# A trunk layer on one core: two output-projection blocks run together, and two norms moved into the middle of feed-forward blocks

## The chip, the cores and the metric

The kernel runs on one core of a Trainium2 chip. The metric is the device time of one execution in microseconds (us), the median over several runs. The core has five engines that work side by side, each through its own instructions in a fixed order: TensorE (PE) multiplies matrices, VectorE (DVE), ScalarE (ACT) and GpSimd (POOL) do elementwise work, and SyncE (SP) issues most of the transfers (DMA) between the chip's memory and the core's own.

## The reference, cut to what matters

The layer mixes three branches into `merged`, projects it, and adds the normed result to `x`; a second norm feeds a gated feed-forward network with a causal convolution of width three. The change touches the last lines of the mixer and the first ones of the network:

```python
def rms_norm(x, g):
    y = x * lax.rsqrt(jnp.mean(x * x, axis=-1, keepdims=True) + NORM_EPS)
    return y * g

merged = gates[:, :, 0] * y_pool + gates[:, :, 1] * y_rwkv + gates[:, :, 2] * y_mem
x = x + rms_norm(merged @ w_o[l], norm_mix_post[l])          # projection, residual norm
h = rms_norm(x, norm_ffn_pre[l])                             # next norm
u = causal_dwconv(h @ w_ffn_up[l], conv_w[l], conv_b[l])     # feed-forward, up
u_gate, u_val = jnp.split(u, 2, axis=-1)
f = (jax.nn.gelu(u_gate, approximate=True) * u_val) @ w_ffn_down[l]
x = x + rms_norm(f, norm_ffn_post[l])
```

The sequence has 1024 rows, `x` has 1024 channels, the feed-forward has 2 x 2816.

## The kernel before, in words

All activations lie transposed: 128 channels on the partitions, 512 positions (a half of the sequence) in a row. A product of float32 accuracy is made of three matmuls on a high and a low part of both factors (`mm3`, lines 163 to 171: the lines L168, L169 and L170 of the profile). A block of 128 output channels for one half takes 8 rows of the contraction (`k` = 0 to 7), so 24 matmuls (`gemm`).

Each block's weights come in four tiles of two `k` each (`load_more`): SP issues a load into a raw buffer (L158), ACT casts it to the high part `whi` (L129), and POOL subtracts to get the low part `wlo` (L132). Blocks take turns between two classes of buffers, each with three raw and four split tiles, so that a block's fourth load has to wait until the first tile's raw buffer has been split. The tile scheduler fixes the order on every engine when the program is built. An engine that waits holds up all that stands behind it, and SP likewise holds up later loads.

The stretch of the program around the change, in order:

- `merge(0)` makes the eight merged rows of the first half. Its last step for a row is a cast by ACT (`mgh`, L122) and a subtraction by DVE (`mgl`, L123).
- `wo_gemm(0)` makes the eight projection blocks of the first half, one after the other. Each reads all eight merged rows, the last one made last.
- `merge(1)`, the residual step and norm of the first half, and `wo_gemm(1)` for the second half follow. `wo_gemm(1)` runs its first two blocks through `two_gemms`: rows 0 to 6 of both, then row 7 of both.
- Then come the feed-forward blocks of the first half. This text calls the first ten of them U0 to U9: channels 0, NF, 1, NF+1, 2, NF+2, 3, NF+3, 4, NF+4 (NF = 22; the ones below NF are gates, `ug`, the others values, `uv`). Each block's result is convolved by one ACT pass (L962) and two DVE passes (L963, L964, with a small copy, L966).
- Between them runs the second half's residual step. `wo_residual(1)` sums squares over channels by a matmul with a matrix of ones (`psn<-ss`, L1148), takes the reciprocal root by two ACT passes (Ln and Exp, L200), and then on each of eight rows `o` DVE scales (L1191), adds `x` (L1193) and, with a square by ACT (L1139, L1142), accumulates the next sum of squares `s2` (L1143); SP stores the row to `d_x1` (L1194). Before, the matmul of this norm stands behind U0.
- `wo_norm(1)` does the same with `s2`: matmul (`psn<-s`, L1148), Ln, Exp, and on each row a scaling by DVE (L1210) and a split into `h2h` and `h2l`. Before, its matmul stands behind U5. Behind it ACT loads its table for gelu (L194), and `up_act` makes gelu times value for the finished pairs and stores them.
- Then come U10 and on: the first blocks of the second half, beside which DVE and ACT make differences and splits of the two halves (`differences`, L1306, L122, L123) that the remaining channels need. Those run as pairs with fewer products (`up_pairs`), followed by the down projection.

Of the kernel before, what the change touches and what calls it, by code (L numbers as in the profile page):

```python
# [20 lines left out]
KC = D // P  # L21
# [7 lines left out]
NF = 22  # L29
# [15 lines left out]
def trunk_kernel(ctx: ExitStack, tc: tile.TileContext, xT, memT, pvec, w_in, w_kv, w_upd, w_upg,  # L45
# [76 lines left out]
        A.copy(hi, src)  # L122
        return (lo_eng or V).tensor_tensor(lo, src, hi.bitcast(F32), op=ALU.subtract)  # L123

    hi_on_act, lo_on_dve, last_whi = [False], [False], [None]

    def split_w(src, hi, lo):
        if hi_on_act[0]:
            last_whi[0] = A.copy(hi, src).ins  # L129
        else:  # L130
            G.tensor_scalar(hi, src, 1.0, 0.0, op0=ALU.mult, op1=ALU.add)
        (V if lo_on_dve[0] else G).tensor_tensor(lo, src, hi.bitcast(F32), op=ALU.subtract)  # L132
# [11 lines left out]
    def load_w(ap, nk, kp=2, c=None):  # L144
        if c is None:
            cls[0] ^= 1
            c = cls[0]
        ps = Ws()
        ps.c = c
        for k0 in range(0, nk, kp):  # L150
            load_more(ps, ap, k0, min(kp, nk - k0), kp)
        return ps
# [17 lines left out]
        last_mm[0] = PE.matmul(ps, wl, xh, start=False, stop=stop).ins  # L170
        return first

    def gemm(ws, rhs, width=512, behind=None, ps=None, log=None):

        if ps is None:
            ps = psg.tile([P, 512], F32, name="psg", tag=f"g{getattr(ws, 'c', 0)}")[:, :width]
        n = len(ws)
        for k in range(n):
            m = mm3(ps, ws[k], rhs(k), k == 0, k == n - 1)
            if k == 0 and behind is not None:  # L180
                later(m, behind)
            if log is not None:
                log.append(last_mm[0])
        return ps


# [6 lines left out]
    def table(name):  # L193
        load = A.preload_act_table_set(name).ins  # L194
        for u in phase[1]:
            tc.add_manual_dep(load, u.name, nosync, reason="table")
        phase[:] = [load, [load]]
# [759 lines left out]
    def conv(j, n, src, d):  # L957

        if n == 0:
            zcs[j] = const.tile([P, 2], F32, name="zc2", tag="zc2", bufs=16)  # L960
        zc = zcs[j]
        A.activation(d, src, AF.Identity, scale=col("cw2", j), bias=col("cb", j))  # L962
        V.scalar_tensor_tensor(d[:, 1:], src[:, :511], col("cw1", j), d[:, 1:], op0=ALU.mult, op1=ALU.add)  # L963
        V.scalar_tensor_tensor(d[:, 2:], src[:, :510], col("cw0", j), d[:, 2:], op0=ALU.mult, op1=ALU.add)  # L964
        if n == 0:
            V.tensor_copy(zc, src[:, 510:512])  # L966
        else:
            V.scalar_tensor_tensor(d[:, 0:1], zc[:, 1:2], col("cw1", j), d[:, 0:1], op0=ALU.mult,
                                   op1=ALU.add)
            V.scalar_tensor_tensor(d[:, 0:2], zc, col("cw0", j), d[:, 0:2], op0=ALU.mult, op1=ALU.add)  # L970
# [4 lines left out]
        cnt[e] = (cnt[e] + 1) % 4  # L975
        return pmp.tile([P, 512], F32, name=name, tag=f"n{8 + 4 * e + cnt[e]}")

    def up_block(j, n, ws):
        e = j // NF
        d = work(e, ("ug", "uv")[e])  # L980
        conv(j, n, gemm(ws, lambda k: (h2h[n][:, k], h2l[n][:, k])), d)
        return d

    def up_act(i, n, ug, uv):
# [172 lines left out]
    def wo_gemm(n, js):  # L1157
        s = slice(n * 512, n * 512 + 512)
        for j in js:
            if j == 0:  # L1160
                o = [(ow if n == 0 else ow1).tile([P, 2, 512], F32, name="o", tag=f"q{4 * n + a}") for a in range(4)]
                os_.append([o[k // 2][:, k % 2] for k in range(KC)])
                sss.append(ow.tile([P, 512], F32, name="ss", tag="ss", bufs=2))
            rhs = lambda k: (mgh[k][:, s], mgl[n][k])
            if n == 1 and j == 0:
                two.extend(two_gemms([load_w(w_o[e], KC) for e in range(2)], rhs, KC - 1))
            ps = two.pop(0) if two else gemm(load_w(w_o[j], KC), rhs)
            V.tensor_copy(os_[n][j], ps)
            if n == 1 and j > 4:
                sq = wp.tile([P, 512], F32, name="sq", tag="st", bufs=3)  # L1170
                V.tensor_tensor(sq, os_[n][j], os_[n][j], op=ALU.mult)
                V.tensor_tensor(sss[n], sss[n], sq, op=ALU.add)
            else:
                sumsq(sss[n], ps, j == 0, V)

    def wo_residual(n, after=None):

        s = slice(n * 512, n * 512 + 512)
        o = os_[n]
        rs = norm(ow, sss[n], after)  # L1180
        s2 = ow.tile([P, 512], F32, name="s2", tag="ss", bufs=2)
        if n:
            xts = hf.tile([P, KC, 512], F32, name="xts", tag="h2h1")
            SP.dma_start(xts, xT[:, s].rearrange("(k p) t -> p k t", p=P))
        for k in range(KC):
            if n:
                xt = xts[:, k]
            else:
                xt = ow.tile([P, 512], F32, name="xt", tag="xt", bufs=2)
                SP.dma_start(xt, xT[k * P:(k + 1) * P, s])  # L1190
            V.scalar_tensor_tensor(o[k], o[k], col("g_mix_post", k), rs, op0=ALU.mult,  # L1191
                                   op1=ALU.mult)
            V.tensor_tensor(o[k], o[k], xt, op=ALU.add)  # L1193
            SP.dma_start(d_x1[k][:, s], o[k])  # L1194
            sumsq(s2, o[k], k == 0, V)
            if k % 2:
                yield s2
# [6 lines left out]
    def wo_norm(n, s2, after=None):  # L1204

        o = os_[n]
        rs = norm(ow, s2, after)
        new_h2()
        for k in range(KC):
            V.scalar_tensor_tensor(o[k], o[k], col("g_ffn_pre", k), rs, op0=ALU.mult,  # L1210
                                   op1=ALU.mult)
            split(o[k], h2h[n][:, k], h2l[n][:, k], V)
            if k % 2:
                yield
# [24 lines left out]
    for _ in wo_norm(0, s2, last_mm[0]):  # L1239
        pass  # L1240
    wo_gemm(1, range(2, 8))
    def first(j):
        return up_block(j, 0, load_w(w_fup[j], KC))

    pairs = [[first(0)]]
    res = wo_residual(1, last_mm[0])
    s2 = next(res)
    pairs[0].append(first(NF))
    s2 = next(res)
    for i in (1, 2):  # L1250
        pairs.append([first(i)])
        s2 = next(res, s2)
        pairs[i].append(first(NF + i))
        s2 = next(res, s2)

    ahead = [load_w(w_fup[3], KC), load_w(w_fup[NF + 3], KC)]
    steps = wo_norm(1, s2, last_mm[0])
    next(steps)
    table(GELU)
    later(phase[0], last_whi[0], True)  # L1260
    for n in range(4):
        j = (3, NF + 3, 4, NF + 4)[n]
        d = up_block(j, 0, ahead.pop(0))
        if n < 2:
            ahead.append(load_w(w_fup[(4, NF + 4)[n]], KC))
            up_act(n, 0, *pairs[n])
            pairs.append([d])
        else:
            up_act(n, 0, *pairs[n]) if n == 2 else None
            pairs.append([d])  # L1270
        if n < 3:
            next(steps)
    up_act(3, 0, pairs[3][0], pairs[4][0])
    up_act(4, 0, pairs[5][0], pairs[6][0])


    o0, o1 = os_
# [389 lines left out]
```

## Time and profile before

| what | value |
|---|---|
| median of 3 runs | 2056.73 us (2052.93 to 2056.75) |
| the profiled execution's own time | 2058.67 us |
| span of its profile | 2056.8 us |
| mean granted clock of TensorE | 0.995 |
| merged rows of the first half, last subtraction ends | 1241.37 us |
| projection blocks of the first half, first matmul | 1232.85 us |
| U0, first matmul | 1371.35 us |
| matmul of the second half's residual norm | 1376.79 us |
| matmul of its next norm | 1408.79 us |

The profile is one execution. A row of the timeline gives the start in us from the span's start, the duration, engine, line, operation and tiles; `x4` merges four equal instructions in a row, and brackets give the engine's idle time before it and what ended that. A row of the table by stretches gives the stretch's length, then for each engine its busy time and number of instructions, the share of its clock that TensorE was granted (PEclk), and the DMA share and rate. Busy time of PE overstates, because matmuls overlap: their rate is read from their starts.

### The profile page before, as it was taken

What the parts mean: (1) busy time and instruction counts of PE and PEld (TensorE: products, weight loads), DVE (VectorE), ACT (ScalarE), POOL (GpSimd) and SP (SyncE); (2) the same over time, 40 slices, a digit from 0 to 9 for tenths busy, and PEclk for the clock granted to TensorE, in tenths of its full rate; (3) what the DMA queues carried; (4) which work ended last, traced back from release to release, by engine and by line L of the source; (5) the groups of instructions that cost most, each with busy time, mean ns of one, the idle gap of its engine ahead of it and who ended that gap; (6) DMA issues with size and microseconds to landing.
All of it is one profiled execution on the core that took longest, in us unless ns stands there. A gap on an engine that the chain in (4) does not pass through costs nothing. (4 is left out here: it accounts for less than half of the span.)

```text
span 2056.8 us, 34070 instructions
## 1 busy us (share of the span) xinstructions
PE 2000.2 (97%) x12246; PEld 1558.2 (76%) x12246; DVE 1378.4 (67%) x2204; ACT 1073.6 (52%) x2249; POOL 804.4 (39%) x883
## 2 busy tenths in 40 slices
PE   8999999999999999999999999999999999999997
PEld 5777767786778667776778887877678888877886
DVE  6567537663568357734596552768889888867798
ACT  7575338723773358434567343545544554444544
POOL 4521213121222121111122355655579888832441
PEclk9999999999999999999999999999999999999999
DMA  4412112120212121212525543645332222169776
GB/s 152 136 42 75 66 36 86 58 93 22 88 62 83 36 90 40 90 63 89 193 92 189 157 136 106 191 129 164 97 95 87 85 80 82 67 198 260 166 183 150
DMA packets 176714, 221.84 MB, mean 108 GB/s; under 512 B 16544, under 2 KB 128288, under 8 KB 176544
## 3 DMA queue, kind: packets, MB, share of 16 engines
q1 hardware_dynamic: 163616, 204.44, 30.7%
q0 software_dynamic: 11856, 14.16, 4.2%
q8 instruction: 97, 1.59, 0.3%
q10 hardware_dynamic: 1072, 1.05, 0.2%
q14 instruction: 73, 0.60, 0.1%
HBM read 170.30 MB, written 49.28 MB: 107 GB/s over the span
## 5 line engine op out<-in xcount | busy, mean ns | idle before, releaser
L132 POOL TENSOR_TENSOR wlo<-wraw,whi 128x256 fp32r<-128x256 f32 x472 | 412.7, 884 | 940.7 <-ACT whi L129 774.5
L168 PE MATMUL psg<-hh,whi 128*128 128x512 f32 x928 | 380.1, 410 | 2.6 <-DVE kv L315 2.6
L170 PE MATMUL psg<-hh,wlo 128*128 128x512 f32 x928 | 376.3, 406 | 0.4
L169 PE MATMUL psg<-hl,whi 128*128 128x512 f32 x928 | 375.5, 405 | 0.0
L129 ACT CAST whi<-wraw 128x256 fp32r<-128x256 f32 x472 | 182.5, 403 | 227.6 <-PE psg L169 105.7
L168 PEld LDWEIGHTS psg<-hh,whi 128*128 128x128 f32 x928 | 174.6, 188 | 43.1 <-DVE kv L315 3.8
L170 PEld LDWEIGHTS psg<-hh,wlo 128*128 128x128 f32 x928 | 174.2, 188 | 43.2 <-POOL wlo L132 5.9
L169 PEld LDWEIGHTS psg<-hl,whi 128*128 128x128 f32 x928 | 174.6, 188 | 39.4 <-issue 3.6
L1011 POOL TENSOR_TENSOR wt<-a,wt 128x256 fp32r<-128x256 f32 x136 | 156.7, 1176 | 35.6 <-ACT wt L1010 35.6
L168 PE MATMUL psd<-f,u 128*128 128x512 f32 x292 | 114.7, 393 | 3.1 <-ACT u L1405 2.4
L169 PE MATMUL psd<-f,u 128*128 128x512 f32 x292 | 114.6, 393 | 0.6 <-DVE f L1409 0.6
L170 PE MATMUL psd<-f,u 128*128 128x512 f32 x292 | 114.1, 392 | 0.0
L170 PE MATMUL psf<-h2h,wt 128*128 128x512 f32 x272 | 105.9, 389 | 1.0 <-POOL wt L1011 1.0
L169 PE MATMUL psf<-h2l,wt 128*128 128x512 f32 x272 | 105.8, 389 | 0.0
L168 PE MATMUL psf<-h2h,wt 128*128 128x512 f32 x272 | 105.8, 389 | 0.0
L1025 DVE SCALAR_TENSOR_TENSOR d<-z,pv,d 128x1023 f32<-128x1023 f32 x68 | 101.1, 1491 | 2.2
L1011 POOL TENSOR_TENSOR wt<-s,wt 128x256 fp32r<-128x256 f32 x68 | 80.3, 1201 | 3.4 <-ACT wt L1010 2.1
L686 DVE TENSOR_TENSOR HV<-ph,Hd 64x128 f32<-64x128 f32 x112 | 32.4, 289 | 72.2 <-PE ph L640 48.1
L168 PE MATMUL psf<-t,wt 128*128 128x512 f32 x204 | 79.4, 389 | 0.0
L169 PE MATMUL psf<-t,wt 128*128 128x512 f32 x204 | 79.4, 389 | 0.0
L170 PE MATMUL psf<-t,wt 128*128 128x512 f32 x204 | 79.4, 389 | 0.0
L1023 ACT ACTIVATE d<-z,pv 128x1024 f32<-128x1024 f32 x34 | 42.4, 1246 | 67.6 <-DVE z L1102 51.9
(425 smaller groups left out, 4747.0 us busy)
## 6 DMA issues: line engine op xcount, KB each, us to landing
wraw<-in_w_in SPq DMA_DIRECT2D x240, 128.0 KB, 2.4
a<-in_w_fup SPq DMA_DIRECT2D x128, 128.0 KB, 2.4
d_zg<-st SPq DMA_DIRECT2D x48, 256.0 KB, 2.7
wraw<-in_w_fup SPq DMA_DIRECT2D x80, 128.0 KB, 2.5
fw<-in_w_fdn SPq DMA_DIRECT2D x33, 256.0 KB, 4.3
fraw<-d_f SPq DMA_DIRECT2D x33, 256.0 KB, 4.5
wraw<-in_w_prwkv SPq DMA_DIRECT2D x64, 128.0 KB, 2.4
wraw<-in_w_o SPq DMA_DIRECT2D x64, 128.0 KB, 2.5
```

The costliest lines, as they stand in the source:

```text
L129: last_whi[0] = A.copy(hi, src).ins
L132: (V if lo_on_dve[0] else G).tensor_tensor(lo, src, hi.bitcast(F32), op=ALU.subtract)
L168: first = PE.matmul(ps, wh, xh, start=start, stop=False)
L169: PE.matmul(ps, wh, xl, start=False, stop=False)
L170: last_mm[0] = PE.matmul(ps, wl, xh, start=False, stop=stop).ins
L686: ready = V.tensor_tensor(HV[q, :, c + 1, e], ph[q], Hd[q], op=ALU.add).ins
L1011: low = eng.tensor_tensor(w[1][:, us], src[u], w[0][:, us].bitcast(F32), op=ALU.subtract)
L1023: A.activation(d, z, AF.Identity, scale=col("cw2", j), bias=col("cb", j))
L1025: V.scalar_tensor_tensor(d[:, n:], z[:, :T - n], col(cw, j), d[:, n:], op0=ALU.mult, op1=ALU.add)
```

## The change

Three things are moved:

1. `wo_gemm(0)` now also takes its first two blocks through `two_gemms`: rows 0 to 6 of both, then row 7 of both.
2. The matmul of the second half's residual norm stands in the middle of U0 (behind the fourth of its eight rows) and that of the next norm in the middle of U5. All that hangs on them is recorded from there: the residual rows are spread over U0 to U4, and `up_act` and the steps of `wo_norm` come one block earlier.
3. Two sets of weight casts are pinned behind the norms on ACT (`hold`): those of U2 behind the Exp of the first norm, those of U7 behind the Exp of the second. The pin of the gelu table behind the last weight cast is gone.

In the changed file lines from 126 on stand three lines lower, and those from 188 on five lower: L200 becomes L205, L1148 becomes L1153.

```diff
-            last_whi[0] = A.copy(hi, src).ins
+            i = A.copy(hi, src)
+            last_whi[0] = i.ins
+            if hold[0] is not None:
+                later(i, hold[0])
...
-    def gemm(ws, rhs, width=512, behind=None, ps=None, log=None):
+    def gemm(ws, rhs, width=512, behind=None, ps=None, log=None, amid=None):
...
+            if amid is not None and k == 3:
+                amid()
...
-            if n == 1 and j == 0:
+            if j == 0:
                 two.extend(two_gemms([load_w(w_o[e], KC) for e in range(2)], rhs, KC - 1))
...
-    pairs = [[first(0)]]
-    res = wo_residual(1, last_mm[0])
-    s2 = next(res)
-    pairs[0].append(first(NF))
-    s2 = next(res)
-    for i in (1, 2):
-        pairs.append([first(i)])
-        s2 = next(res, s2)
-        pairs[i].append(first(NF + i))
-        s2 = next(res, s2)
-
-    ahead = [load_w(w_fup[3], KC), load_w(w_fup[NF + 3], KC)]
-    steps = wo_norm(1, s2, last_mm[0])
-    next(steps)
-    table(GELU)
-    later(phase[0], last_whi[0], True)
+    def begin():
+        res.append(wo_residual(1, last_mm[0]))
+        s2[0] = next(res[0])
+        pins.append(phase[1][-1])
+
+    def end():
+        steps.append(wo_norm(1, s2[0], last_mm[0]))
+        next(steps[0])
+        pins.append(phase[1][-1])
+        table(GELU)
+
+    res, steps, pins = [], [], []
+    first(0, begin)
+    for j in (NF, 1, NF + 1, 2):
+        s2[0] = next(res[0], s2[0])
+        hold[0] = pins[0] if j == 1 else None
+        first(j)
+
+    queue = (NF + 2, 3, NF + 3, 4, NF + 4)
+    ahead = [load_w(w_fup[j], KC) for j in queue[:2]]
+    for n, j in enumerate(queue):
+        blocks.append(up_block(j, 0, ahead.pop(0), None if n else end))
         if n < 3:
-            next(steps)
-    up_act(3, 0, pairs[3][0], pairs[4][0])
-    up_act(4, 0, pairs[5][0], pairs[6][0])
+            hold[0] = None if n else pins[1]
+            ahead.append(load_w(w_fup[queue[n + 2]], KC))
+            hold[0] = None
+            up_act(n, 0, *blocks[2 * n:2 * n + 2])
+            next(steps[0])
+    for n in (3, 4):
+        up_act(n, 0, *blocks[2 * n:2 * n + 2])
```

What the scheduler makes of it is shown by the order of instructions at three places. On PE, before, the first two projection blocks of the first half meet like this (`psg_12561` is the first block's accumulator, `psg_12612` the second's; `mgh7` and `mgl70` are the last merged row):

```order
L170 MATMUL psg_12561<-mgh6_12071,wlo_12557 128x512
L168 MATMUL psg_12561<-mgh7_12072,whi_12556 128x512
L169 MATMUL psg_12561<-mgl70_12529,whi_12556 128x512
L170 MATMUL psg_12561<-mgh7_12072,wlo_12557 128x512
L168 MATMUL psg_12612<-mgh0_12065,whi_12589 128x512
```

On PE, after, with `psg_12585` and `psg_12586` for the two blocks, the end of the second block's row 6 and the two last rows:

```order
L173 MATMUL psg_12586<-mgh6_12071,wlo_12581 128x512
L171 MATMUL psg_12585<-mgh7_12072,whi_12556 128x512
L172 MATMUL psg_12585<-mgl70_12529,whi_12556 128x512
L173 MATMUL psg_12585<-mgh7_12072,wlo_12557 128x512
L171 MATMUL psg_12586<-mgh7_12072,whi_12580 128x512
L172 MATMUL psg_12586<-mgl70_12529,whi_12580 128x512
L173 MATMUL psg_12586<-mgh7_12072,wlo_12581 128x512
```

The last merged row is first read after 42 matmuls and no longer after 21. On ACT, before, the Ln and Exp of the second half's residual norm (`rs`) stand behind eight weight casts, four of U1 (`whi_14026` to `whi_14044`) and four of U2 (`whi_14093` to `whi_14111`), and behind the convolution pass of U0:

```order
L129 CAST whi_14038<-wraw_14037 128x256
L129 CAST whi_14044<-wraw_14043 128x256
L129 CAST whi_14093<-wraw_14092 128x256
L129 CAST whi_14099<-wraw_14098 128x256
L129 CAST whi_14105<-wraw_14104 128x256
L129 CAST whi_14111<-wraw_14110 128x256
L962 ACTIVATE ug_13976<-psg_13977,pv_83 128x512
L200 ACTIVATE rs_14009<-psn_14007,eps_111 128x512
L200 ACTIVATE rs_14009<-rs_14009 128x512
```

On ACT, after, U1's four casts are `whi_14038` to `whi_14056` and U2's first three `whi_14105` to `whi_14117`:

```order
L129 CAST whi_14050<-wraw_14049 128x256
L129 CAST whi_14056<-wraw_14055 128x256
L205 ACTIVATE rs_13992<-psn_13990,eps_111 128x512
L205 ACTIVATE rs_13992<-rs_13992 128x512
L129 CAST whi_14105<-wraw_14104 128x256
L129 CAST whi_14111<-wraw_14110 128x256
L129 CAST whi_14117<-wraw_14116 128x256
L967 ACTIVATE ug_13976<-psg_13977,pv_83 128x512
```

U2's casts and U0's convolution now stand behind the Exp; U1's fourth cast still stands ahead of the Ln. At the second norm on ACT, before, the last cast ahead is U7's fourth (`whi_14379`), and U5's convolution (`uv_14305`) stands ahead too:

```order
L129 CAST whi_14379<-wraw_14378 128x256
L962 ACTIVATE uv_14305<-psg_14306,pv_83 128x512
L200 ACTIVATE rs_14386<-psn_14384,eps_111 128x512
L200 ACTIVATE rs_14386<-rs_14386 128x512
L194 ACT_TABLE_LOAD
```

On ACT, after, `whi_14324` is U6's fourth cast, `ug_14250` U4's convolution, `uv_14329` U5's, and `whi_14375` U7's first cast:

```order
L129 CAST whi_14324<-wraw_14323 128x256
L967 ACTIVATE ug_14250<-psg_14251,pv_83 128x512
L205 ACTIVATE rs_14345<-psn_14343,eps_111 128x512
L205 ACTIVATE rs_14345<-rs_14345 128x512
L199 ACT_TABLE_LOAD
L122 CAST h2h1_14348<-o_13493 128x512 x2
L967 ACTIVATE uv_14329<-psg_14330,pv_83 128x512
L129 CAST whi_14375<-wraw_14374 128x256
```

U7's four casts have moved from ahead of the second norm to behind its table load and the first two rows' casts.

More of the change, by code (lines that the diff above doesn't have):

```diff
@@ L123, in split @@
         return (lo_eng or V).tensor_tensor(lo, src, hi.bitcast(F32), op=ALU.subtract)
-    hi_on_act, lo_on_dve, last_whi = [False], [False], [None]
+    hi_on_act, lo_on_dve, last_whi, hold = [False], [False], [None], [None]
     def split_w(src, hi, lo):
         if hi_on_act[0]:
-            last_whi[0] = A.copy(hi, src).ins
+            i = A.copy(hi, src)
+            last_whi[0] = i.ins
+            if hold[0] is not None:
+                later(i, hold[0])
         else:
@@ L976, in work, with up_block @@
         return pmp.tile([P, 512], F32, name=name, tag=f"n{8 + 4 * e + cnt[e]}")
-    def up_block(j, n, ws):
+    def up_block(j, n, ws, amid=None):
         e = j // NF
         d = work(e, ("ug", "uv")[e])
-        conv(j, n, gemm(ws, lambda k: (h2h[n][:, k], h2l[n][:, k])), d)
+        conv(j, n, gemm(ws, lambda k: (h2h[n][:, k], h2l[n][:, k]), amid=amid), d)
         return d
@@ L1241, in trunk_kernel, with first @@
     wo_gemm(1, range(2, 8))
-    def first(j):
-        return up_block(j, 0, load_w(w_fup[j], KC))
-    pairs = [[first(0)]]
-    res = wo_residual(1, last_mm[0])
-    s2 = next(res)
-    pairs[0].append(first(NF))
-    s2 = next(res)
-    for i in (1, 2):
-        pairs.append([first(i)])
-        s2 = next(res, s2)
-        pairs[i].append(first(NF + i))
-        s2 = next(res, s2)
-    ahead = [load_w(w_fup[3], KC), load_w(w_fup[NF + 3], KC)]
-    steps = wo_norm(1, s2, last_mm[0])
-    next(steps)
-    table(GELU)
-    later(phase[0], last_whi[0], True)
[L1261 to L1270, printed above, removed]
-        if n < 3:
-            next(steps)
-    up_act(3, 0, pairs[3][0], pairs[4][0])
-    up_act(4, 0, pairs[5][0], pairs[6][0])
+    blocks, s2 = [], [None]
+    def first(j, amid=None):
+        blocks.append(up_block(j, 0, load_w(w_fup[j], KC), amid))
+    def begin():
[17 more added lines that the diff above has]
+        blocks.append(up_block(j, 0, ahead.pop(0), None if n else end))
+        if n < 3:
+            hold[0] = None if n else pins[1]
[5 more added lines that the diff above has]
+        up_act(n, 0, *blocks[2 * n:2 * n + 2])
     o0, o1 = os_
```

## The prediction

> **What bounds the kernel now.** I read the page first, then the waits of PE, then the busy times by stretch, and in each of three stretches the timeline of the engine that PE waits for. One line of the page:
>
> ```profile
> PE 2000.2 (97%) x12246; PEld 1558.2 (76%) x12246; DVE 1378.4 (67%) x2204; ACT 1073.6 (52%) x2249; POOL 804.4 (39%) x883
> ```
>
> PE is busy nearly throughout, so only time in which it waits, or runs slowly, can be won. Among the longest waits of PE over the whole span (total, times, longest) are these:
>
> ```profile
> PE psn L1148 <- DVE s L1143: 3.1, 1, 3.1
> PE psg L170 <- POOL wlo L132: 3.0, 5, 1.6
> PE psg L168 <- ACT whi L129: 2.2, 4, 1.3
> ```
>
> The first is the next norm's wait for `s2`; the others lie nearly all in the stretch behind that norm. A wait of 2.93 at the first projection block is shown in part 1. Five stretches, by busy time (length, PE, PEld, DVE, ACT, POOL, PEclk, DMA share, GB/s):
>
> ```profile
> 1232.85:1248.84 15.99, 12.90 (x49) 9.98 (x48) 4.00 (x5) 7.54 (x17) 8.02 (x12) 0.89 0.35 106
> 1371.35:1376.79 5.44, 5.44 (x25) 4.50 (x24) 2.08 (x3) 1.33 (x4) 3.74 (x6) 1.00 0.40 115
> 1385.04:1408.74 23.70, 20.33 (x89) 16.09 (x87) 23.59 (x34) 11.39 (x25) 14.24 (x15) 0.99 0.52 168
> 1405.57:1416.60 11.03, 7.96 (x28) 5.72 (x28) 4.63 (x9) 4.30 (x12) 5.67 (x8) 0.85 0.68 213
> 1416.60:1475.00 58.40, 53.00 (x214) 38.39 (x213) 56.85 (x78) 35.40 (x76) 35.50 (x36) 1.00 0.34 104
> ```
>
> The second row is U0 undisturbed: 24 matmuls in 5.44 us, 0.2267 us each. (Counts hold the one at the edge too.) The first row is the first two projection blocks, 48 matmuls, worth 10.88 us: 5.11 us are lost there. The fourth is the second norm and U6, worth 0.87 for the norm's matmul (below) and 5.44: 4.7 us lost. The fifth is worth 213 x 0.2267 = 48.3: 10.1 us lost, and DVE is busy 56.85 of 58.40. In the third, the residual step, DVE is never free.
>
> **Part 1, the projection blocks.** How the last merged row becomes late:
>
> ```profile
> 1237.21 0.73 POOL L132 TENSOR_TENSOR wlo<-wraw,whi 128x256 fp32r<-128x256 f32 x1 [1.06 <-ACT whi L129]
> 1237.38 0.39 PE L170 MATMUL psg<-mgh,wlo 128*128 128x512 f32 x1
> 1238.73 1.28 ACT L194 ACT_TABLE_LOAD   x1
> 1240.03 0.62 ACT L122 CAST mgh<-g 128x512 fp32r<-128x512 f32 x1
> 1240.68 0.69 DVE L123 TENSOR_TENSOR mgl<-g,mgh 128x512 fp32r<-128x512 f32 x1 [3.98 <-ACT mgh L122]
> 1240.70 0.56 PE L168 MATMUL psg<-mgh,whi 128*128 128x512 f32 x1 [2.93 <-ACT mgh L122]
> 1242.01 0.63 PE L170 MATMUL psg<-mgh,wlo 128*128 128x512 f32 x1
> 1246.41 2.92 POOL L132 TENSOR_TENSOR wlo<-wraw,whi 128x256 fp32r<-128x256 f32 x4 [3.08 <-ACT whi L129]
> ```
>
> PE stops at 1237.6 for a cast that stands on ACT behind a table load, and its matmuls then take 0.63 us, not 0.39: the row's clock is 0.89. After the change PE has the second block's rows 0 to 6 left, 21 matmuls or 4.76 us, and comes to the last row at 1242.4; the row is whole at 1241.37, 1.0 us earlier. ACT's order up to that cast is the same. What must be ready instead is the second block's weights: its last `wlo` ends at 1237.94, where PE needs it at 1242. The third block starts at 1243.73 and no longer at 1248.84. Its fourth tile, due 18 matmuls later at 1247.8, is the first of the four splits from 1246.41, done near 1247.15; three splits of the fourth block now go ahead of it on POOL, which was idle for 3.08 us there and takes 3 x 0.73 for them. Gain 5.1; between 4.4, should that tile come 0.7 late, and 5.1.
>
> **Part 2, the wait at the second norm.** The rows of the first norm and of its follow-up, on ACT, then DVE, then PE:
>
> ```profile
> 1378.18 1.33 ACT L129 CAST whi<-wraw 128x256 fp32r<-128x256 f32 x4 [3.61 <-DMA wraw<-in_w_fup]
> 1382.40 0.41 ACT L129 CAST whi<-wraw 128x256 fp32r<-128x256 f32 x1 [2.89 <-DMA wraw<-in_w_fup]
> 1382.71 0.78 ACT L962 ACTIVATE ug<-psg,pv 128x512 f32<-128x512 f32 x1
> 1383.39 0.68 ACT L200 ACTIVATE rs<-psn,eps 128x512 f32<-128x512 f32 x1
> 1384.09 0.63 ACT L200 ACTIVATE rs<-rs 128x512 f32<-128x512 f32 x1
> ```
> ```profile
> 1383.52 0.75 DVE L963 SCALAR_TENSOR_TENSOR ug<-psg,pv,ug 128x511 f32<-128x511 f32 x1 [9.83 <-ACT ug L962]
> 1385.04 1.89 DVE L1191 SCALAR_TENSOR_TENSOR o<-o,pv,rs 128x512 f32<-128x512 f32 x2
> 1406.93 1.80 DVE L1143 TENSOR_TENSOR s<-s,sq 128x512 f32<-128x512 f32 x2
> ```
> ```profile
> 1376.79 1.02 PE L1148 MATMUL psn<-ss,ones 128*128 128x512 f32 x2
> 1377.89 0.40 PE L169 MATMUL psg<-h2l,whi 128*128 128x512 f32 x1
> 1408.79 2.08 PE L1148 MATMUL psn<-s,ones 128*128 128x512 f32 x2 [3.07 <-DVE s L1143]
> 1411.82 0.40 PE L168 MATMUL psg<-h2h,whi 128*128 128x512 f32 x1
> ```
>
> The norm's matmul costs 1377.89 - 1376.79 - 0.23 = 0.87. Its result was there by 1378, but Ln stood behind U2's fourth cast, which waited for its load until 1382.40, and behind U0's convolution. After the change Ln stands behind U1's fourth cast, the first of the four from 1378.18, still a wait for a load. So the matmul, though 2.7 us earlier, gains nothing itself; Ln starts at 1378.18 + 0.31 = 1378.5, Exp ends at 1378.5 + 0.70 + 0.63 = 1379.8, and DVE begins at 1379.9, 5.1 earlier.
>
> From there DVE works without a gap, 23.7 us before, to 1408.7. By the built order U0's convolution (1383.52 to 1385.04, 1.5) now falls inside, and the second half of U3's (0.8) behind the last sum: `s2` is whole at 1408.7 - 5.1 + 1.5 - 0.8 = 1404.3. POOL has about the same 15 splits beside it. PE, undisturbed, is in the middle of U5 at 1371.35 + 5.5 x 5.44 + 0.87 = 1402.1. So I expect the wait not to go but to shrink from 3.07 to about 2.2, now inside U5. Before, U6 followed directly; now twelve matmuls (2.72) remain. Gain (1408.8 - 1404.3) - 2.7 = 1.8. Bounds: 0.4 if DVE is 1.4 slower, as it may be where it meets more splits; 5.4 if `s2` is ready in time (U7 would start at 1402.1 + 0.87 + 2.72 + 5.44 = 1411.2, not 1416.6).
>
> One cost stays open, the slow matmuls after a wait: before, 1408.79 to 1411.82 is 3.03 us for the norm and three matmuls, worth 0.87 + 0.68, so 1.5 are lost. Elsewhere:
>
> ```profile
> 75.30 0.50 PE L168 MATMUL psg<-gl 128*128 128x512 f32 x1 [2.45 <-ACT st L325]
> 75.64 0.40 PE L169 MATMUL psg<-gl 128*128 128x512 f32 x1
> 1848.20 0.50 PE L168 MATMUL psd<-f,u 128*128 128x512 f32 x1 [2.38 <-ACT u L1405]
> 1849.53 0.63 PE L168 MATMUL psd<-f,u 128*128 128x512 f32 x1
> ```
>
> After 2.45 us of idling there are none, after 2.38 there are. I keep the 1.5, a cost that the gain of 1.8 leaves as it was. The Trainium skill, "TensorE: Matmul & The Clock Gate", section "Part 1: The HAM clock gate", says that the clock is halved after a window of about 3.4 us without work, and that the window runs freely. By its length alone a wait of 2.2 us would cost no clock, and the gain of this part would be 3.3, not 1.8; this trace's 0.63 us matmuls after 2.38 and 2.93 us speak against counting on it.
>
> **Part 3, what follows the second norm.** Before:
>
> ```profile
> 1415.99 0.41 ACT L129 CAST whi<-wraw 128x256 fp32r<-128x256 f32 x1 [4.66 <-DMA wraw<-in_w_fup]
> 1417.69 0.63 ACT L200 ACTIVATE rs<-rs 128x512 f32<-128x512 f32 x1
> 1418.34 1.28 ACT L194 ACT_TABLE_LOAD   x1
> ```
> ```profile
> wraw<-in_w_fup SPq DMA_DIRECT2D x80, 128.0 KB, 2.5
> ```
>
> Exp ended at 1418.32, since U7's fourth cast waited ahead of it. Now U6's fourth cast is ahead. Its load stands on SP behind the store of the last residual row and can go when U6's first tile is split, about when `s2` is whole; I take 1404.6. With 2.5 us to landing (the page's median, quoted last) as the fast bound and the 4.66 us of that last wait as the slow one, the cast is at 1407.1 to 1409.3; the cast, U4's convolution, Ln and Exp take 0.31 + 0.78 + 0.68 + 0.63 = 2.4. Exp ends at 1409.5 to 1411.7, mid 1410.6, 7.7 earlier. PE is 1.8 earlier, so DVE, of which the stretch behind is full, has 5.9 us more lead. ACT waited there (1417 to 1477) mainly for DVE:
>
> ```profile
> ACT t L122 <- DVE o L1306: 11.1, 8, 4.1
> ```
>
> Weight casts stand behind those casts of differences, and PE waits for the weights. The lead caps the gain at 5.9 of the 10.1 us that are lost there; waits for POOL (1.6 the longest) need not go. I take 3.4, a little over half of the cap. The bounds are 5.9 and -1, a loss by the hold. That is U7's weights, now behind the Exp: table 1.28, two casts of rows at 0.62, U5's convolution 0.78, the cast 0.41, the split 0.73, so the first pair of tiles is there at 1410.6 + 4.4 = 1415.0. U7 starts at 1404.3 + 0.87 + 1.5 + 2.72 + 5.44 = 1414.8 and reads the low part two matmuls later, at 1415.3. A margin of 0.3: no cost in the middle, up to 0.8 at the slow bound.
>
> **Sum.** 5.1 + 1.8 + 3.4 = 10.3. The profiled execution took 2058.67, so it would take 2048.4; it lies 1.94 above the median of the runs shown, so the median would be 2046.4 against 2056.73.
>
> **The rivals.** Only the projection gains (0.2): the static orders trade one wait for another behind U5, parts 2 and 3 are nothing. For: DVE is full there whatever the order, and ACT has as many rows to wait for. Against: DVE's start at both norms comes earlier by more than PE does. 2056.73 - 5.1 = 2051.6. The residual step is hidden whole (0.17): `s2` by 1402.1, if fewer of DVE's passes are slowed. Eight of its passes took 946 ns in the mean, one alone 0.67 us:
>
> ```profile
> L1193 DVE TENSOR_TENSOR o<-o,xts 128x512 f32<-128x512 f32 x8 | 7.5, 946 | 0.0
> ```
> ```profile
> 1393.36 0.67 DVE L1193 TENSOR_TENSOR o<-o,xts 128x512 f32<-128x512 f32 x1
> ```
>
> Eight passes at 0.67 alone would win 2.2 us, just enough. Then 5.1 + 5.4, and 3 of part 3: 2043.2. The change doesn't do what it says (0.03): third block starved after the pair, part 1 returned: 2056.7. Slower (0.05): the hold starves U7. Each us that Exp is later than 1410.9 is a us of PE. At 1418.3, as before, PE would wait 7.4 and lose the 5.1 + 1.8 again; with part 3 at nothing and 2 us of slow clock after the wait the time is 2059. More than 0.2% slower it is from an Exp at 1420: 2061. For: that Exp was held by a load before. Against: the load now ahead of it is an older one.
>
> **The numbers.** My forecast has 0.55: 2046.4. A measurement of this kernel tells 0.2% or 4.1 us from no change, so faster means below 2052.6: nearly all of my case, the hidden one, and half of the first rival, 0.83; same 0.11; slower 0.06. The range reaches from the hidden case, less 1.7, 2041.5, to 2053.5, the first rival with part 1 at its low end and the spread of the runs.
>
> **What would show it.** Right: no wait at the last merged row and the third projection block 5.1 earlier after its start; Ln directly behind a cast that waits for a load; `psn<-s` still waiting about 2 us on DVE inside U5; Exp to gelu table some 8 us earlier; fewer waits for `whi` behind it. Wrong: PE waiting for `wlo` in U7, no wait at `psn<-s`, or the same 10 us lost in the stretch behind U6.

## The result, and the profile after

The changed kernel takes 2047.03 us (median of 4 runs, 2046.09 to 2048.95), the kernel before, beside it on the same chip, 2056.4 us (4 runs, 2052.93 to 2056.75). The ratio is 0.9955, with a 95% interval of 0.9943 to 0.9967: 9.3 us less, between 6.8 and 11.7. The profiled execution took 2047.03 us with a span of 2045.3, 11.5 less than the span of before. The forecast was a median of 2046.4 with 10.3 us gained. The total is right; two of its three terms are not.

Where the span became shorter, read from the starts of matmuls in both profiles:

| stretch | before | after | difference | predicted |
|---|---|---|---|---|
| up to the first projection block | 1232.85 | 1232.52 | -0.3 | 0 |
| part 1: first to third projection block | 15.99 | 10.88 | -5.1 | -5.1 |
| third projection block to U0 | 122.51 | 123.00 | +0.5 | 0 |
| U0 to U5 | 28.11 | 28.12 | 0 | 0 |
| part 2: U5 to U7, with the second norm | 17.13 | 18.24 | +1.1 | -1.8 |
| part 3: U7 to the first pair of channels (psf) | 82.32 | 75.45 | -6.9 | -3.4 |
| psf to the end | 557.90 | 557.07 | -0.8 | 0 |

Three of these stretches of before, by busy time as in the prediction's table (the residual step from the first norm's Exp to the second norm's matmul, U5 to U7, and U7 to psf), were these:

```profile
1384.72:1408.79 24.07, 20.65 (x90) 16.36 (x88) 23.91 (x34) 11.71 (x27) 14.29 (x15) 0.99 0.52 168
1399.46:1416.59 17.13, 13.71 (x51) 9.88 (x50) 10.74 (x18) 6.46 (x15) 8.61 (x12) 0.90 0.64 198
1416.59:1498.91 82.32, 76.28 (x314) 56.87 (x312) 73.59 (x114) 46.92 (x102) 47.55 (x51) 1.00 0.34 104
```

The busy times over the whole of after, and the same stretches with the two projection blocks ahead:

```profile
PE 1998.1 (98%) x12246; PEld 1560.0 (76%) x12246; DVE 1378.4 (67%) x2204; ACT 1071.9 (52%) x2249; POOL 799.9 (39%) x883
```

```profile
1232.52:1243.40 10.88, 10.88 (x50) 9.01 (x48) 3.80 (x5) 6.17 (x14) 6.62 (x9) 1.00 0.35 107
...
1374.94:1400.82 25.88, 22.46 (x100) 18.26 (x98) 25.71 (x34) 13.55 (x32) 15.12 (x17) 0.98 0.53 173
1394.52:1412.76 18.24, 14.82 (x52) 11.02 (x50) 13.97 (x24) 12.06 (x25) 7.90 (x10) 0.81 0.53 166
1412.76:1488.21 75.45, 73.52 (x313) 57.59 (x312) 66.27 (x104) 41.34 (x93) 44.72 (x52) 1.00 0.36 114
```

The projection row has PE busy for its whole 10.88 us at a clock of 1.00. The residual step became longer, 25.88 and not 24.07. U5 to U7 became longer too, at a clock of 0.81. In the last row DVE has 66.27 us of work where it had 73.59: 7.3 less, nearly the 6.9 by which the row is shorter.

**Part 1.** ACT and POOL around the last merged row, after:

```profile
1237.71 1.28 ACT L199 ACT_TABLE_LOAD   x1
1239.01 0.62 ACT L122 CAST mgh<-g 128x512 fp32r<-128x512 f32 x1
```
```profile
1242.04 0.39 PE L171 MATMUL psg<-mgh,whi 128*128 128x512 f32 x1
```
```profile
1240.01 5.12 POOL L135 TENSOR_TENSOR wlo<-wraw,whi 128x256 fp32r<-128x256 f32 x7 [2.89 <-PE psg L172]
```

The row is cast behind the table load as before, and PE first reads it at 1242.04, the 43rd matmul, without a wait. POOL splits seven tiles in a row from 1240.01 and is in time for the third block.

**Part 2.** The first norm on ACT, after, and the second on PE:

```profile
1373.28 0.41 ACT L129 CAST whi<-wraw 128x256 fp32r<-128x256 f32 x1 [3.08 <-DMA wraw<-in_w_fup]
1373.60 0.69 ACT L205 ACTIVATE rs<-psn,eps 128x512 f32<-128x512 f32 x1
1374.31 0.63 ACT L205 ACTIVATE rs<-rs 128x512 f32<-128x512 f32 x1
```
```profile
1400.82 2.08 PE L1153 MATMUL psn<-s,ones 128*128 128x512 f32 x2 [3.42 <-DVE s L1148]
...
1403.12 0.63 PE L172 MATMUL psg<-h2l,whi 128*128 128x512 f32 x1
...
1406.11 0.63 PE L173 MATMUL psg<-h2h,wlo 128*128 128x512 f32 x1
```

Ln stands behind the one cast that waits for a load, as foreseen. PE then waits 3.42 us for `s2`, and runs matmuls of 0.63 us until 1406.5. From the norm's matmul to U7 it takes 1412.76 - 1400.82 = 11.94 us for work worth 0.87 + 2.72 + 5.44 = 9.03: 2.9 us lost to the slow clock.

**Part 3.** The second norm on ACT, after:

```profile
1404.48 0.40 ACT L129 CAST whi<-wraw 128x256 fp32r<-128x256 f32 x1 [3.53 <-DMA wraw<-in_w_fup]
1404.79 0.77 ACT L967 ACTIVATE ug<-psg,pv 128x512 f32<-128x512 f32 x1
1405.46 0.68 ACT L205 ACTIVATE rs<-psn,eps 128x512 f32<-128x512 f32 x1
1406.17 0.63 ACT L205 ACTIVATE rs<-rs 128x512 f32<-128x512 f32 x1
...
1409.84 1.01 ACT L129 CAST whi<-wraw 128x256 fp32r<-128x256 f32 x3
```

Exp ends at 1406.80, 6.0 us ahead of U7's first matmul (1412.76). Before, it ended 1.7 us behind it (1418.32 against 1416.59). U7's casts, held behind Exp, start at 1409.84 and U7 does not wait for them. The waits of PE over the whole span, after:

```profile
PE psn L1153 <- DVE s L1148: 3.4, 1, 3.4
...
PE psg L173 <- POOL wlo L135: 1.6, 3, 0.8
```

Waits for `wlo` in `psg` were 3.0 us in 5, now 1.6 in 3; those of 2.2 us for `whi` have left the top of the list.

### The profile page after: what moved, and what is told of

The parts are those of the page before. It is cut to its first block, busy times and chain, and to the rows that moved or that the text cites. A ratio compares the mean times of both kernels' runs of the same rounds, so it can differ in the third digit from the quotient of the medians.

```text
span 2045.3 us, 34063 instructions
## 1 busy us (share of the span) xinstructions
PE 1998.1 (98%) x12246; PEld 1560.0 (76%) x12246; DVE 1378.4 (67%) x2204; ACT 1071.9 (52%) x2249; POOL 799.9 (39%) x883
## 4 chain that ended last, share of the span: by engine, by line
PE 40%; DVE 6%; DMA 3%; issue 1%; ACT 1%; POOL 1%; SPq 1%; POOLq 0%; ACTq 0%; DVEq 0%
PE psg L173 5%; PE psg L171 5%; PE psg L172 5%; PE psf L171 5%; PE psf L173 5%; PE psf L172 5%; PE psd L172 2%; PE psd L173 2%; PE psd L171 2%; DMA R<-d_f 1%; POOL wlo L135 1%; DMA fw<-in_w_fdn 1%; DVE o L1215 1%; DMA wraw<-in_w_fup 1%; DVE h2l L123 1%
```

## The experiments

Two theories on part 3 were set against each other. **Head start**: the stretch behind the second norm is bound by DVE's remaining work, and the gain is the earlier Exp. **New order**: the gain is the changed sequence on ACT and DVE there (`up_act` one block earlier, other neighbours), whenever Exp comes. On part 2: the wait is set by when DVE starts and how fast its passes are, or by something else. Times between marks are from each kernel's own profile, since the programs reach the first projection block up to 4.4 us apart (1230.1 to 1234.5). A profile is one execution and can lie off the median: e2's took 2047.68 us where the median of its runs is 2054.42, e1's 2053.49 where it is 2050.02.

| kernel | ratio to before, 95% | first Exp to `psn<-s` | wait there | U5 to U7 | second Exp's end less U7's start | U7 to psf | DVE busy in it | second Exp to psf |
|---|---|---|---|---|---|---|---|---|
| before | 1 | 24.07 | 3.07 | 17.13 | +1.7 | 82.32 | 73.59 | 80.6 |
| after | 0.9955 [0.9943, 0.9967] | 25.88 | 3.42 | 18.24 | -6.0 | 75.45 | 66.27 | 81.4 |
| e1_proj_only | 0.9978 [0.9969, 0.9987] | 24.07 | 3.48 | 18.37 | -0.1 | 80.63 | 72.04 | 80.8 |
| e2_norms_only | 0.9977 [0.9966, 0.9988] | 25.48 | 2.60 | 16.23 | -3.5 | 77.41 | 69.19 | 80.9 |
| e5_ln_first | 0.9942 [0.9927, 0.9957] | 26.05 | 0.20 | 12.53 | -3.5 | 77.49 | 69.39 | 81.0 |
| e9_ln2_first | 0.9939 [0.9923, 0.9956] | 25.89 | 2.80 | 16.43 | -8.2 | 74.47 | 66.09 | 82.7 |
| e8_exp_late | 0.9961 [0.9947, 0.9975] | 25.92 | 2.78 | 14.83 | +1.1 | 79.13 | 71.31 | 78.1 |
| e10_both_ln | 0.9923 [0.9908, 0.9938] | 25.69 | none | 11.88 | -6.6 | 75.29 | 67.08 | 81.9 |
| e7_head8 | 0.9971 [0.9961, 0.9981] | 25.52 | 2.62 | 16.78 | -3.8 | 80.82 | 74.40 | 84.7 |
| e12_no_low | one run | 21.89 | none | 11.79 | -6.6 | 74.28 | 66.23 | 80.9 |

**e1_proj_only: part 1 alone.** Only this line of the change is made:

```diff
-            if n == 1 and j == 0:
+            if j == 0:
```

> The kernel before with the projection pair of the first half alone; both norms stand where they stood. Head start (part 3's gain is the earlier Exp of the second norm, which lets DVE start earlier against PE) and new order (it is the changed static order behind that norm) expect the same here: the third projection block 5.1 us earlier, up to 0.5 of it lost again by U0, the second norm's wait still 3 us, the stretch from U7 to the first pair of channels (psf) still 82.3 us. In all 4.5 to 5.1 us less than before, ratio 0.9975. A ratio under 0.9965 would mean that the pair helps the later parts too, one over 0.9985 that it does not last.

Measured 0.9978, 4.5 us. The two projection blocks of this kernel:

```profile
1232.60:1243.48 10.88, 10.88 (x49) 9.01 (x48) 3.79 (x5) 6.32 (x14) 6.93 (x10) 1.00 0.37 115
```

The same 10.88 us as in the changed kernel: 5.1 us by the profile, and U0 comes 5.2 earlier. Part 1 stands alone and holds. Its size depends on the execution of before: in e2, which has before's order at the projection blocks, PE waited 2.08 us there and not 2.93, no slow matmuls followed, and the two blocks took 13.73 us, 2.85 more than 10.88.

Behind it, U5 to U7 and U7 to psf of this kernel:

```profile
1394.22:1412.59 18.37, 14.89 (x51) 11.08 (x50) 11.79 (x19) 8.20 (x18) 8.76 (x11) 0.81 0.58 184
1412.59:1493.22 80.63, 75.03 (x313) 57.31 (x312) 72.04 (x113) 45.13 (x99) 46.88 (x50) 1.00 0.33 106
```

Both theories expected 82.3 us for the second row, and it is 1.7 less. From U0 to psf, ACT, DVE and POOL carry out the same instructions in the same order here as in before. What differs is above all that PE lost 1.5 us more to the slow clock ahead of U7, and Exp ends 0.1 us ahead of U7 and not 1.7 behind it. This is an equal order with another Exp, and the stretch is shorter by nearly the 1.9 us by which Exp comes earlier against U7: head start accounts for it, new order does not.

**e2_norms_only: the changed kernel without part 1.** The same line turned back.

> The changed kernel without the projection pair of the first half. If the parts add up, all that lies behind the third projection block is the changed kernel's, later by 4.9 to 5.4 us: psn<-s waits 2.8 to 3.4 us inside U5, U5 to psf is 93 to 94 us, ratio to before 0.9965 to 0.998. If the pair is what lets the norms gain (through the state of loads and queues behind it), U5 to psf is over 96 us and the ratio 0.999.

Measured 0.9977, 4.7 us, at the low end of the gain that was expected. U5 to psf is 16.23 + 77.41 = 93.64 us, the changed kernel's 93.69. The two ratios multiply to 0.9955: the parts add. The wait of 2.60 is a little under what was expected, and no slow matmuls followed it. U5 to U7 is 2.0 us shorter than in the changed kernel, and U7 to psf, in the same order of ACT, DVE and POOL, 2.0 longer: PE came earlier and Exp did not, and nothing was won. 1.8 of the 2.0 are waits in U7 for weights behind the hold (it takes 7.24 us, not 5.44), and U7 itself had begun 1.1 us late for such a wait.

**e5_ln_first: no load ahead of the first norm's Ln.** U1's fourth cast is held behind the first Exp as well:

```diff
-            if hold[0] is not None:
+            if skip[0] > 0:
+                skip[0] -= 1
+            elif hold[0] is not None:
                 later(i, hold[0])
...
-        hold[0] = pins[0] if j == 1 else None
+        hold[0] = pins[0] if j in (NF, 1) else None
+        skip[0] = 3 if j == NF else 0
```

> The changed kernel with one more cast behind the first norm's Exp: U1's fourth, whose wait for its load held up Ln. ACT's order differs by this one cast, SP's by two places, the other engines' not at all. If the wait at the second norm is set by when DVE starts the residual rows: the first Exp ends 3.0 to 3.4 us earlier (1371.5 to 1371.9 and not 1374.9), s2 is whole 3 us earlier (near 1397.6), psn<-s waits under 0.7 us instead of 3.42, no slow matmuls follow, and U6 begins 5 to 5.6 us earlier. If it is set by POOL's splits or by something else than the start, s2 moves by under 1.5 us and the wait stays over 2. Behind it, head start: PE is 5 to 5.6 earlier but the second Exp only about 3, so some 1 to 2 of it are lost again by psf; 3.5 to 4.5 us less than the changed kernel, ratio to before 0.9935. New order: all of the 5 to 5.6 stay, ratio 0.9928. If the load of U6's fourth tile does not come earlier with the last row's store, Exp stays and U7 starves by 3.5: gain 0 to 2.

ACT at the first norm, PE at the second, then the busy times of U5 to U7 and of U7 to psf:

```profile
1368.52 0.69 ACT L207 ACTIVATE rs<-psn,eps 128x512 f32<-128x512 f32 x1 [0.55 <-PE psn L1155]
1369.24 0.63 ACT L207 ACTIVATE rs<-rs 128x512 f32<-128x512 f32 x1
```
```profile
1395.93 1.12 PE L1155 MATMUL psn<-s,ones 128*128 128x512 f32 x2 [0.20 <-DVE s L1150]
```
```profile
1392.85:1405.38 12.53, 12.21 (x52) 9.12 (x50) 8.27 (x14) 8.18 (x16) 3.81 (x5) 1.00 0.57 171
1405.38:1482.87 77.49, 73.89 (x312) 57.77 (x313) 69.39 (x110) 43.96 (x99) 47.35 (x54) 1.00 0.34 112
```

Ln now waits for the norm's matmul, no longer for a load. Counted from U0, Exp ends at 5.1 us and not at 8.5, 3.4 earlier. The residual step lasts 26.05 us as in the changed kernel, the wait shrinks by 3.2 to 0.20, and no slow matmuls follow: U5 to U7 takes 5.7 us less. So DVE's start sets this wait. But of the 5.7 us only 3.7 are left at psf: the second Exp comes only 3.2 us earlier against U5, and the stretch from U7 grows by 2.0, with DVE's work in it. That is what head start expected; new order expected 5 to 5.6. The ratio, 0.9942, can't tell the two apart. Nor does this kernel show that it is DVE's work that binds, since 1.8 of the 2.0 are the hold's price, as in the forecast's rival: U7 waits for late low parts and takes 7.24 us, not 5.44.

```profile
1411.57 0.50 PE L175 MATMUL psg<-h2h,wlo 128*128 128x512 f32 x1 [1.00 <-POOL wlo L137]
```

**e9_ln2_first: no load ahead of the second norm's Ln.** U6's fourth tile is loaded and cast behind the second Exp:

```diff
-    ahead = [load_w(w_fup[j], KC) for j in queue[:2]]
+    ahead = [load_w(w_fup[queue[0]], KC), load_w(w_fup[queue[1]], KC - 2)]
...
             hold[0] = None if n else pins[1]
+            if n == 0:
+                load_more(ahead[0], w_fup[queue[1]], KC - 2, 2, 2)
```

> The changed kernel with U6's fourth cast behind the second norm's Exp, so that Ln need not wait for that cast's load; PE's and POOL's orders are the same, ACT's and DVE's differ by a few neighbours. U7 begins where it did (1412.8), Exp ends 3 to 3.8 us earlier (1403.0 to 1403.8 and not 1406.8). Head start: the stretch from U7 to psf, 75.45 us for 13 blocks that are worth 70.7, gets 2 to 3.5 us shorter; ratio to before 0.9940 to 0.9945. New order: the head start is worth nothing, the stretch stays at 75.5 within 0.5, ratio 0.9955.

ACT at the second norm, and U7 to psf:

```profile
1399.31 0.69 ACT L205 ACTIVATE rs<-psn,eps 128x512 f32<-128x512 f32 x1 [0.36 <-PE psn L1153]
1400.03 0.63 ACT L205 ACTIVATE rs<-rs 128x512 f32<-128x512 f32 x1
```
```profile
1408.89:1483.36 74.47, 72.88 (x314) 57.84 (x312) 66.09 (x104) 40.61 (x91) 45.42 (x51) 1.00 0.35 114
```

Counted from U5, Exp ends 4.1 us earlier. It leads U7 by only 2.2 us more (8.2 and not 6.0), since U7 comes earlier too, and the stretch is 1.0 shorter. Head start had expected 2 to 3.5, new order at most 0.5: the lead is still worth something, but less and less, with 13 blocks worth 70.7 us in a stretch of 74.5. The ratio, 0.9939, has more in it than this: U5 to U7 took 1.8 less than in the changed kernel.

**e8_exp_late: the hold turned round.** U7's four casts are put ahead of the second Ln, as before the change; the rest stays:

```diff
         next(steps[0])
+        later(phase[1][-2], last_whi[0], True)
...
-    ahead = [load_w(w_fup[j], KC) for j in queue[:2]]
+    ahead = [load_w(w_fup[j], KC) for j in queue[:3]]
...
-            hold[0] = None if n else pins[1]
-            ahead.append(load_w(w_fup[queue[n + 2]], KC))
-            hold[0] = None
+            if n:
+                ahead.append(load_w(w_fup[queue[n + 2]], KC))
```

> The changed kernel with the second hold turned round: U7's four casts stand ahead of the second norm's Ln, as before the change; both matmuls stay amid U0 and U5, and up_act stays one block earlier. Exp ends 4.5 to 6.5 us later than in the changed kernel (1411.3 to 1413.3). Head start: the stretch from U7 to psf gets 4 to 6 us longer (79.5 to 81.5 us), ratio to before 0.9975 to 0.9985. New order: the stretch stays within 1 us of 75.45, ratio 0.9955 to 0.996. U7 itself is not starved in either.

ACT at the second norm, and U7 to psf:

```profile
1406.11 0.41 ACT L129 CAST whi<-wraw 128x256 fp32r<-128x256 f32 x1 [2.69 <-PE psg L173]
1406.42 0.69 ACT L205 ACTIVATE rs<-psn,eps 128x512 f32<-128x512 f32 x1
...
1407.66 0.63 ACT L205 ACTIVATE rs<-rs 128x512 f32<-128x512 f32 x1
```
```profile
1407.21:1486.34 79.13, 74.86 (x313) 58.81 (x312) 71.31 (x114) 46.51 (x101) 46.21 (x51) 0.98 0.32 106
```

Against U5, Exp is 3.6 us later than in the changed kernel (4.5 to 6.5 were expected), and the stretch 3.7 us longer: head start in kind, just under its range in size, and outside the 1 us of new order. The ratio of 0.9961 would fit new order; it comes from elsewhere. The wait was 0.6 us shorter here and no slow matmuls followed it, so U5 to U7 took 3.4 us less, and the two nearly cancel. This is the one kernel that needs clearly less than 80 us from Exp to psf, 78.1. The scheduler rearranged ACT's and DVE's neighbours with this edit, so its order is neither before's nor the changed kernel's: an order with `up_act` one block earlier and no hold may be worth 2 to 3 us, which these runs do not settle.

**e7_head8: eight needless passes of DVE.** They stand between the second Exp and the first normed row:

```diff
         rs = norm(ow, s2, after)
+        for _ in range(8 * n):
+            V.tensor_tensor(rs, rs, rs, op=ALU.max)
```

> The changed kernel with eight needless passes of DVE on the reciprocal root of the second norm (its maximum with itself, 128x512, so no value changes) ahead of the first normed row: DVE has 5.4 us (8 x 0.67) to 8 us more to do there, ACT's Exp, the hold and all matmuls stay. Head start (the stretch behind U7 lasts as long as DVE's remaining work plus 8 to 9 us in which DVE waits): U7 to psf is 80 to 83 us and not 75.45, DVE's busy time in it 71 to 74 and not 66.3, ratio to before 0.998 to 0.9995. New order: 75.5 to 77 us, ratio 0.9955 to 0.9965.

U7 to psf:

```profile
1413.54:1494.36 80.82, 74.51 (x314) 57.40 (x312) 74.40 (x117) 43.70 (x97) 49.11 (x53) 1.00 0.34 108
```

DVE's busy time in it grew by 8.1 and the stretch by 5.4, inside the range of head start and far over that of new order: PE pays for work that is given to DVE. It does not pay in full. Exp is only 3.8 us ahead of U7 here and not 6.0, which by itself lengthens the stretch; counted from Exp, psf comes 3.3 us later (84.7 against 81.4), for eight passes that keep DVE busy for 7.0. DVE waits 6.4 us in the stretch, where head start had 8 to 9. The scheduler also put other passes of DVE and ACT in another order, so the 3.3 are not the passes' alone. The ratio, 0.9971, lies between the two expectations, since U5 to U7 took 1.5 us less than in the changed kernel and head start's upper sizes did not come.

**e12_no_low: no subtractions by POOL beside the residual step.** The low parts of U2's to U6's weights are left out:

```diff
-        lo = wp.tile([P, kp, P], FR, name="wlo", tag=f"wlo{ps.c}", bufs=4)
+        lo = hi if no_low[0] else wp.tile([P, kp, P], FR, name="wlo", tag=f"wlo{ps.c}", bufs=4)
...
+        if not no_low[0]:
+            (V if lo_on_dve[0] else G).tensor_tensor(lo, src, hi.bitcast(F32), op=ALU.subtract)
...
+        no_low[0] = j != NF
...
+    no_low[0] = False
```

Without them these products are less accurate, so this kernel only shows where the time goes.

> The changed kernel without the low parts of U2's to U6's weights: POOL's 20 subtractions are left out, and the third matmul of each product takes the high part instead, so the count of matmuls is the same. If the residual step is long because DVE's passes are slowed while POOL subtracts, it shrinks from 25.9 us (Exp of the first norm to psn<-s) to 20 to 22 us, nearly all passes of L1196 take 0.65 to 0.7 us, and psn<-s does not wait. If it is long by DVE's own work and its waits for ACT or loads, it stays over 25 us and psn<-s waits about 3 us.

The groups of DVE's residual passes, with count, busy time and mean, in the changed kernel and in this one (scaling, adding `x`, sum of squares):

```profile
L1198 DVE TENSOR_TENSOR o<-o,xts 128x512 f32<-128x512 f32 x8 | 8.5, 1066 | 0.0
L1148 DVE TENSOR_TENSOR s<-s,sq 128x512 f32<-128x512 f32 x7 | 6.9, 992 | 0.1
L1196 DVE SCALAR_TENSOR_TENSOR o<-o,pv,rs 128x512 f32<-128x512 f32 x8 | 6.7, 864 | 6.2 <-ACT rs L205 6.2
```
```profile
L1198 DVE SCALAR_TENSOR_TENSOR o<-o,pv,rs 128x512 f32<-128x512 f32 x8 | 5.7, 747 | 6.6 <-ACT rs L207 6.6
L1200 DVE TENSOR_TENSOR o<-o,xts 128x512 f32<-128x512 f32 x8 | 5.4, 685 | 0.0
L1150 DVE TENSOR_TENSOR s<-s,sq 128x512 f32<-128x512 f32 x7 | 4.8, 685 | 0.1
```

The last of these sums in this kernel:

```profile
1395.07 0.69 DVE L1150 TENSOR_TENSOR s<-s,sq 128x512 f32<-128x512 f32 x1
```

The passes together fall from 22.1 to 15.9 us, though the scaling ones take 0.75 us, a little over the 0.65 to 0.7 expected. `s2` is whole 20.3 us after Exp (1375.44 to 1395.76), 1.6 us before PE asks for it at 1397.33, and nothing waits. (The table's 21.89 for this kernel ends at PE's matmul.) So the residual step has 6.2 us of DVE's passes slowed beside POOL's, and is 5.6 us shorter without them (20.3 against 25.9).

**e10_both_ln: e5 and e9 together.**

> Both casts that held up an Ln are behind the Exp: U1's fourth at the first norm (as in e5) and U6's fourth at the second (as in e9). If the gains come from DVE's starts at both norms, they add: psn<-s waits 0.2 us without slow matmuls as in e5, Exp ends some 2.3 us earlier than in e5, so that U7, which lost 1.8 us to late low parts in e5, loses under 0.5, and the stretch from U7 to psf is 74 to 76 us. From U5 to psf that is 87 to 88.5 us, against 93.69 in the changed kernel and 90.02 in e5; ratio to before 0.9915 to 0.993. If only the order counts, U5 to psf stays at 90 us as in e5, ratio 0.994.

U5 to U7 and U7 to psf:

```profile
1394.82:1406.70 11.88, 11.88 (x51) 9.31 (x50) 11.21 (x20) 11.03 (x23) 6.54 (x8) 1.00 0.61 185
1406.70:1481.99 75.29, 73.08 (x313) 57.90 (x312) 67.08 (x104) 40.95 (x92) 46.26 (x52) 1.00 0.36 115
```

The ratio is 0.9923 [0.9908, 0.9938], which lies wholly below the changed kernel's interval: this version is faster than before and than the changed kernel, about 0.3% less than the changed one. The intervals of e5 and e9 alone overlap the changed kernel's. PE does not wait at the second norm, Exp is 6.6 us ahead of U7, and U5 to psf takes 87.17 us, as expected. U7 still waits 0.64 us for a low part and takes 6.37 us, 0.9 over its worth where under 0.5 was expected.

## Why the prediction was right, and where it was not

**Part 1** was right in size and in each step: no wait, the third block 5.1 us earlier after its start, POOL's splits in time. The 5.1 us hold against before's profile, with its wait and the slow matmuls behind it; against e2's execution, which had no slow matmuls there, they would be 2.85. The half microsecond given back ahead of U0 is within the spread of the profiles: that stretch takes 122.51 to 123.46 us in the kernels shown, and 122.55 to 123.46 among those that have the pair.

**Part 2** missed, -1.8 expected and +1.1 measured against before's profile, while its mechanism held. The start of DVE was right: 1374.98, or 1379.92 in before's times (4.94 later), against 1379.9. Two terms failed. The first is that "POOL has about the same 15 splits beside it": there were 17, in a step that was also 1.8 us longer (POOL was busy for 15.12 of 25.88 us, and for 14.29 of 24.07 before), and DVE's passes were slowed more. The groups of before for scaling and sums were these:

```profile
L1191 DVE SCALAR_TENSOR_TENSOR o<-o,pv,rs 128x512 f32<-128x512 f32 x8 | 7.6, 983 | 0.0
...
L1143 DVE TENSOR_TENSOR s<-s,sq 128x512 f32<-128x512 f32 x7 | 5.6, 805 | 0.1
```

With the 7.5 us of the additions they sum to 20.7, against 22.1 after: 1.4 us, and the norm's matmul came 1.5 us later than forecast (1405.76 in before's times against 1404.3). The second is the slow clock, kept at 1.5 us and measured at 2.9. The sum is the 2.9 us between forecast and result. The bound of 0.4 in the prediction had the first term in it, but not the second. The second is not the change's own: e1, with before's order at this norm, lost 3.0 us to the slow clock (9.28 us from the norm's matmul to U7 for work worth 6.31) and took 18.37 us from U5 to U7. Against e1 the changed kernel gains 0.1 us there, so the sign of part 2 is that of two single executions; that the 1.8 were not won stands against both. e5 and e12 show what was there to win: U5 to U7 in 12.5 and 11.8 us.

The Trainium skill, "SBUF — State Buffer", section "Who interferes with whom", says that a DVE instruction with two inputs in SBUF contends with a GpSimd instruction that reads SBUF. The trace agrees: 685 ns a pass in e12 against 992 and 1066 beside POOL's splits, while the convolution's passes, with one input in `psg`, took 0.74 us in both.

**Part 3** was right in mechanism, and the forecast had half its size: 3.4 expected, 6.9 measured. Two steps of it were off. The lead of DVE was taken as 5.9 us and was 7.7: PE was 2.9 later than forecast, Exp 1.1 (1411.74 in before's times against 1410.6, at the slow bound). And the value of a microsecond of lead was taken as "a little over half"; it was 6.9 / 7.7, or 0.9. The table's last column shows the pattern: whatever PE does before, psf follows the second Exp by 80.6 to 82.7 us in eight of the ten kernels, and DVE's work in the stretch plus 7.8 to 9.2 us of its waits is the stretch's length in nine of ten (e7, with its added passes, has 6.4). So most of what PE lost in part 2 came back as lead in part 3. The end was set by when Exp was done behind the second norm: in e2 and e5 mostly through the weights held behind Exp; in before and e1, where none are held, DVE's work is what starts there, and e7 shows that PE pays for such work. Parts 2 and 3 together gained 5.8 us, against 5.2 predicted. That this is close is partly luck: at 0.9 a us the forecast lead of 5.9 us would have given 5.3 and not 3.4, and the later Exp took about 1.0 back.

The rival that the hold starves U7 did not happen in the changed kernel, but its price was real where PE came earlier (e5, e2: Exp only 3.5 ahead of U7, which then took 1.8 us more). The rival that the static order only trades waits is refuted by the result. No share of the new order in part 3 shows: from before to e1, in one order, the stretch shrank by 1.7 us for 1.9 of lead; from e1 to the changed kernel, across the change of order, by 5.2 for 5.8, the same 0.9 a us. That before's order would have gone on at this rate with still more lead was not run, and e8 leaves 2 to 3 us for an order with `up_act` earlier and no hold; this stays open.

## What to carry to other kernels

Where two engines take turns in being late, do not add up the gains of one of them: find the event that releases the later engine's work (here the second Exp; DVE idled for only about 8 of the 75 to 82 us between U7 and psf), and forecast the end from its time. A normalization that stands in order behind a weight cast waits for that cast's load; here moving its matmul earlier won nothing by itself, and the gain came from which casts stand ahead of it on ACT and whose loads stand ahead on SP. Passes that read two operands beside another engine's passes should be costed with the overlap they will have after the change.

## What was not expected of the hardware

A wait of PE for 2.78 us (e8) had no slow matmuls behind it, one of 2.80 (e9) at the same place had some:

```profile
1398.04 1.13 PE L1153 MATMUL psn<-s,ones 128*128 128x512 f32 x2 [2.78 <-DVE s L1148]
...
1399.23 0.39 PE L172 MATMUL psg<-h2l,whi 128*128 128x512 f32 x1
```
```profile
1398.14 1.12 PE L1153 MATMUL psn<-s,ones 128*128 128x512 f32 x2 [2.80 <-DVE s L1148]
...
1399.59 0.63 PE L173 MATMUL psg<-h2h,wlo 128*128 128x512 f32 x1
```

Behind the one of 3.42 us in the changed kernel 2.9 us were lost. In e9 the norm's matmul to U7 took 10.75 us for work worth 9.03, 1.7 lost; in e8 9.17, 0.1 lost. So two waits of the same length cost nothing and 1.7 us: the length alone does not tell the price. The granted clock does. It is at half in these two stretches, of the changed kernel and of e9:

```profile
1399.82:1406.64 6.82, 5.82 (x12) 3.93 (x13) 2.58 (x6) 3.26 (x8) 3.03 (x4) 0.50 0.77 228
```
```profile
1399.53:1402.94 3.41, 3.41 (x9) 2.63 (x8) 3.27 (x7) 3.35 (x5) 0.53 (x1) 0.50 0.72 209
```

In e8 it stays at 1.00 from the norm's matmul to U7. The loss is half of the time that PE works at half clock: 3.41 / 2 = 1.7 in e9, and (6.82 - 1.0) / 2 = 2.9 in the changed kernel, where the wait lasted 1.0 us into the stretch. In e9 the half clock begins 1.4 us after the wait has ended.

The Trainium skill, "TensorE: Matmul & The Clock Gate", section "Part 1: The HAM clock gate", has the window run freely, and e8 against e9 agrees with that. That the clock is halved only after an idle window of about 3.4 us does not agree with e9, where 2.80 us were enough.
